# A fused decoder layer on one core: the opening's residual moved to ScalarE's queue, in a fixed order, with the first weight tiles in halves

## The chip, the cores and the metric

The kernel runs on one core of a Trainium2 chip. The metric is the device time of one launch in microseconds. A core has TensorE (matrix products, "PE"; its weight loads are listed as "PEld"), VectorE ("DVE"), ScalarE ("ACT"), GpSimd ("POOL") and SyncE ("SP"), which here only issues transfers. Each engine works through its own instructions in order and waits on semaphores; a transfer is issued by an engine's queue and carried out by 16 transfer engines that all queues share.

## What is computed

The reference is one inference step of a decoder layer over a group of 512 prompt tokens and 8 sequences of 8 sample tokens, 576 tokens in all, in float32. It has three sub-layers: a SwiGLU feed-forward block, a mixing block of attention and a state-space scan, and a second feed-forward block. The change lies ahead of and inside the first block:

```python
mod = (jax.nn.silu(c) @ w_ada + b_ada).reshape(bsz, N_SUB, 3, D_MODEL)
shift, scale, gate = mod[:, :, 0], mod[:, :, 1], mod[:, :, 2]
h = _modulate(x, g_pre[0], shift[:, 0], scale[:, 0])      # rms_norm(x, g) * (1 + scale) + shift
f = _swiglu(h, w_ffn_gate[0], w_ffn_up[0], w_ffn_down[0]) # (silu(h @ w_gate) * (h @ w_up)) @ w_down
x = x + FFN_RES * gate[:, 0][:, None] * rms_norm(f, g_post[0])
```

## The kernel before

Activations are kept with the 1024 features on partitions: `xT` is a tile of 128 partitions x 8 feature blocks x 576 tokens, worked on in two halves of 288 tokens (`HALF`). Products in float32 are made from three products of rounded parts: an operand is split into hi (a cast, on ScalarE) and lo (the remainder, a subtraction on VectorE or GpSimd), and `mm3` multiplies hi by hi, hi by lo and lo by hi. A weight tile `wraw` of 128 x 1024 is loaded by SP, cast to `whi` and subtracted to `wlo` by `weights()` (L148 on). That function counts its calls in `wcount`, and where `pool_weights` is set, which holds for the middle of the kernel, it gives the lo part of every second tile to GpSimd.

The opening works towards the first products of the first feed-forward block. SP loads `cT`, constants `cst`, the first half of `xT` in 8 pieces, three small constants, and then the conditioning weights `wada`, 8 pieces of 128 x 512 for each half of a modulation vector. The squares of `xT` are summed over the feature blocks (ScalarE squares, GpSimd adds, VectorE makes the last addition), a product with ones adds them over the partitions, and root and reciprocal follow in `rnorm`. Meanwhile `ada_half(1, 0, 2)` (L338 on) multiplies silu(c) by half of the scale's weights, in eight groups of four small products, transposes the result and writes the factors `A0` for four feature blocks. `prescale` (L463 on) then makes a scaled tile `pm` per feature block on VectorE, its cast `xh` on ScalarE and its remainder `xl` on VectorE or GpSimd.

`Split.half0` loads and splits the first three weight tiles whole, calls `then` (in the code `second`: the other half of the scale, the other four feature blocks, and sixteen steps of `shift`), and runs the 72 products of the three tiles, feature block by feature block. `shift` is a thread of its own: it loads the second half of `xT` and makes the 16 groups of products of the shift vector. Further weight tiles follow through `gemm` (L203 is its product line).

The order of each engine's instructions is set by a scheduler, which places what is not inside a block of `in_order()` by its own choice; inside such a block the order of the code holds between the block's own instructions. The order of SP's loads is the order in which the code calls `load`. The transfers' semaphores go round in eight, so that an issue can only go out when the transfer eight before it has landed.

Of the kernel before, what the change touches and what calls it, by code (L numbers as in the profile page):

```python
# [8 lines left out]
F32 = mybir.dt.float32  # L9
F32R = mybir.dt.float32r  # L10
# [26 lines left out]
def _layer(ctx, tc, A, O, tap, stop):  # L37
# [24 lines left out]
    def load(out, in_):  # L62
        in_queue([nc.sync.dma_start(out=out, in_=in_).ins])  # L63
# [40 lines left out]
    def const(name, shape, dt=F32, src=None):  # L104
        t = cp.tile(shape, dt, tag=name, name=name)
        load(t, A[name] if src is None else src)
        return t

    def f32(ap):
        return ap.bitcast(F32)  # L110

    def sub(out, a, b, pool=False):
        (G if pool else V).tensor_tensor(out, a, b, ALU.subtract)  # L113
# [25 lines left out]
    def run(g):  # L139
        for _ in g:  # L140
            pass
# [156 lines left out]
    class Split:  # L298
# [7 lines left out]
        def half0(self, first=True, last=True):  # L306
            if first:
                flush()
            kc, xh, xl, few = self.kc, self.xh, self.xl, self.first
            self.w = w = [weights(src, kc) for src, _ in self.tiles[:few]]  # L310
            if self.then:
                self.then()
            if few:
                ps = [mmt() for _ in range(few)]
                for k in range(kc):
                    for n in range(few):
                        mm3(ps[n][:, :HALF], *w[n][k], xh(k, 0), xl(k, 0), k == 0, k == kc - 1)
                for n in range(few):
                    self.tiles[n][1](0, 0, ps[n][:, :HALF])
            n0 = len(self.tiles) - self.keep  # L320
            for n, (src, evac) in enumerate(self.tiles[few:], few):
                w.append(weights(src, kc, n0 - self.far <= n < n0 or n in self.spare))
                gemm(None, kc, xh, xl, evac, (0,), w=w[-1])
                yield
            if last:
                flush()
# [127 lines left out]
            V.reciprocal(self.ps, self.ps)  # L454
            return self.ps

    def xsums(x, i):
        o = i * HALF
        s = Sums(NQ)
        for q in range(NQ):  # L460
            s.add(x[:, q, o:o + HALF])
        return s

    def prescale(x, rb, Aj, xh, xl, qs):

        for q in qs:
            t = tmp("pm")
            V.scalar_tensor_tensor(t, x[:, q, :HALF], Aj[:, q, 0:1], rb, ALU.mult, ALU.mult)
            S.copy(xh[:, q, :HALF], t)
            sub(xl[:, q, :HALF], t, f32(xh[:, q, :HALF]), q % 2 == 1)  # L470

    def premod(x, rb, Aj, j, xh, xl, i):

# [256 lines left out]
    load(cT, A["cT"])  # L730
    sq_c = cp.tile([128, 8, 32], F32, tag="sq_c", name="sq_c")
    S.activation(sq_c, cT, AF.Silu)
    cst = const("cst", [128, 448])
    ident, ones = cst[:, 0:128], cst[:, 128:256]
    smask, smask_s = cst[:, 256:384], cst[0:64, 384:448]
    xT, _ = xtile(F32, "xT")
    for q in range(NQ):
        load(xT[:, q, :HALF], A["xT"][:, q, :HALF])
    bada = const("b_ada", [128, 9, 8])
    gpre = const("g_pre", [128, 3, 8])  # L740
    gpost = const("g_post", [128, 3, 8])
    eps_t = cp.tile([128, 1], F32, tag="eps", name="eps_t")
    V.memset(eps_t, EPS)
    identb = cp.tile([128, 128], BF16, tag="identb", name="identb")
    V.tensor_copy(identb, ident)
    A0 = cp.tile([128, 8, 9], F32, tag="A0", name="A0")
    (xh, xhs), (xl, xls) = xtile(F32R, "xh"), xtile(F32R, "xl")
    rbs = [xsums(xT, 0).rnorm(1024.0)]
    run(ada_half(1, 0, 2))
    prescale(xT, rbs[0], A0, xh, xl, range(4))  # L750


    Gs, As = {}, {}
# [38 lines left out]
        V.tensor_tensor(xls[:, :, T:], sh, f32(xhs[:, :, T:]), ALU.subtract)  # L792
        yield from premod(xT, rbs[1], A0, 0, xh, xl, 1)

    def second():

        run(ada_half(1, 1))
        prescale(xT, rbs[0], A0, xh, xl, range(4, 8))
        for _ in range(PRES):
            next(shifts)  # L800
# [4 lines left out]
    look[0] = 1  # L805
    shifts = shift()
    wa = Blocks(xh, xl, lambda q: A["xT"][:, q:q + 2])
    ff = ffn(0, xh, xl, side(), last, wa, 3, (second, again()))
    merge((next(ff), 1), (shifts, SHIFT))
    end = next(ff)  # L810
    xh, xl = X2s
# [1370 lines left out]
```

## Time and profile before

| what | us |
|---|---|
| median of three runs | 1968.27 |
| lowest and highest run | 1964.12, 1970.24 |
| the profiled execution, its own time | 1972.4 |
| its span, first to last instruction | 1970.6 |
| TensorE busy in the span | 1888.8 (96%) |
| VectorE, ScalarE, GpSimd busy | 1433.0, 1027.1, 642.6 |

The busy times are those of the whole span; the opening is the first of 40 slices of it, some 49 us each. In the timeline rows the first two numbers are the start and the duration in us, then engine, line, operation, tiles and shapes, the count of merged instructions, and in brackets the idle time of the engine ahead of them with what ended it.

### The profile page before, as it was taken

The numbers are of one execution on the slowest core, as the hardware profiler recorded it, in microseconds if no ns is written. First come the engines' busy times: TensorE is split into PE (matmuls) and PEld (weight loads), VectorE is DVE, ScalarE is ACT, GpSimd is POOL, SyncE is SP. The second block draws the span as 40 slices with busy tenths as digits, with TensorE's granted clock in tenths as the row PEclk, the third lists the DMA queues.
The fourth block names the chain that finished last, engine by engine and source line by source line (L and its number), as shares of the span: only waits on it lengthen the run. The fifth ranks groups of instructions, "written<-read, shape, count | busy, mean of one in ns | idle before, by whom it ended". The sixth has DMA issues, their size and how long they took to land. (4 is left out here: it accounts for less than half of the span.)

```text
span 1970.6 us, 37005 instructions
## 1 busy us (share of the span) xinstructions
PE 1888.8 (96%) x13779; PEld 1747.8 (89%) x13779; DVE 1433.0 (73%) x2595; ACT 1027.1 (52%) x2247; POOL 642.6 (33%) x645
## 2 busy tenths in 40 slices
PE   6999999999999999999999999999988999999997
PEld 5999898998998999999899778777688999999997
DVE  4887577867785786677667667788866895766875
ACT  4655343556554565455434555655646754534553
POOL 1314234425553242333233111133332422332523
PEclk9999999998999999999999999999999999999999
DMA  9433546354544538355634444378847543232252
GB/s 324 147 111 128 193 134 198 100 188 143 169 133 153 150 95 248 106 174 150 206 120 155 159 138 147 110 259 272 292 164 254 179 166 92 80 100 89 86 178 80
DMA packets 171958, 313.84 MB, mean 159 GB/s; under 512 B 18129, under 2 KB 84402, under 8 KB 171778
## 3 DMA queue, kind: packets, MB, share of 16 engines
q1 hardware_dynamic: 145794, 268.98, 42.6%
q0 software_dynamic: 9088, 34.11, 4.9%
q10 hardware_dynamic: 16896, 8.39, 1.5%
q8 instruction: 108, 1.77, 0.4%
q14 instruction: 72, 0.59, 0.1%
HBM read 284.59 MB, written 26.83 MB: 158 GB/s over the span
## 5 line engine op out<-in xcount | busy, mean ns | idle before, releaser
L113 DVE TENSOR_TENSOR wlo<-wraw,whi 128x512 fp32r<-128x512 f32 (+2 forms) x300 | 336.9, 1126 | 124.7 <-ACT whi L167 94.8
L167 ACT CAST whi<-wraw 128x1024 fp32r<-128x1024 f32 (+2 forms) x264 | 238.0, 905 | 248.1 <-PE mm L203 133.1
L203 PE MATMUL mm<-xh,whi 128*128 128x288 f32 (+1 forms) x1368 | 344.1, 301 | 5.9 <-ACT xh L494 4.4
L203 PE MATMUL mm<-xl,whi 128*128 128x288 f32 (+1 forms) x1368 | 340.8, 298 | 3.2 <-DVE xl L484 2.6
L203 PE MATMUL mm<-xh,wlo 128*128 128x288 f32 (+1 forms) x1368 | 338.1, 296 | 0.2 <-DVE wlo L113 0.2
L203 PEld LDWEIGHTS mm<-xh,whi 128*128 128x128 f32 x1368 | 236.3, 190 | 14.3 <-ACT xh L494 4.6
L203 PEld LDWEIGHTS mm<-xl,whi 128*128 128x128 f32 x1368 | 236.5, 189 | 4.9 <-DVE xl L484 3.3
L203 PEld LDWEIGHTS mm<-xh,wlo 128*128 128x128 f32 x1368 | 236.6, 190 | 0.9 <-DVE wlo L113 0.4
L113 POOL TENSOR_TENSOR wlo<-wraw,whi 128x1024 fp32r<-128x1024 f32 (+1 forms) x60 | 122.0, 2034 | 213.5 <-ACT whi L167 191.3
L203 PE MATMUL mm<-hl,whi 128*128 128x288 f32 x640 | 161.2, 296 | 0.0
L203 PE MATMUL mm<-hh,whi 128*128 128x288 f32 x640 | 160.3, 295 | 0.0
L203 PE MATMUL mm<-hh,wlo 128*128 128x288 f32 x640 | 158.4, 295 | 0.0
L264 PE MATMUL mm<-t,whi 128*128 128x288 f32 x768 | 154.0, 295 | 0.2 <-ACT sg L612 0.2
L264 PE MATMUL mm<-xl,whi 128*128 128x288 f32 x512 | 150.6, 296 | 0.0
L264 PE MATMUL mm<-xh,wlo 128*128 128x288 f32 x512 | 149.0, 295 | 1.5 <-DVE wlo L113 1.5
L264 PE MATMUL mm<-xh,whi 128*128 128x288 f32 x512 | 147.9, 296 | 1.2 <-ACT u L281 0.8
L113 DVE TENSOR_TENSOR wlo<-area,whi 128x512 fp32r<-128x512 f32 x128 | 121.7, 965 | 12.2 <-ACT whi L239 11.6
L264 PEld LDWEIGHTS mm<-t,whi 128*128 128x128 f32 x768 | 122.9, 188 | 2.1 <-ACT whi L239 0.8
L441 POOL TENSOR_TENSOR acc<-acc,sq 128x288 f32<-128x288 f32 x72 | 70.0, 974 | 140.3 <-ACT sq L440 114.1
L203 PEld LDWEIGHTS mm<-hl,whi 128*128 128x128 f32 x640 | 110.8, 188 | 3.5 <-issue 3.4
L203 PEld LDWEIGHTS mm<-hh,whi 128*128 128x128 f32 x640 | 110.6, 188 | 3.5 <-ACT whi L167 1.7
L264 PE MATMUL mm<-t,wlo 128*128 128x288 f32 x384 | 112.6, 295 | 0.0
(443 smaller groups left out, 4666.7 us busy)
## 6 DMA issues: line engine op xcount, KB each, us to landing
wraw<-w_gu SPq DMA_DIRECT2D x108, 512.0 KB, 3.5
craw<-cache SPq DMA_DIRECT2D x128, 320.0 KB, 4.3
wraw<-w_in SPq DMA_DIRECT2D x72, 512.0 KB, 4.4
wada<-w_ada SPq DMA_DIRECT2D x80, 256.0 KB, 4.4
area<-w_ada POOLq DMA_DIRECT2D x16, 1024.0 KB, 6.0
wraw<-w_dn SPq DMA_DIRECT2D x24, 512.0 KB, 4.4
wraw<-w_dn SPq DMA_DIRECT2D x32, 256.0 KB, 2.6
M<-cscr SPq DMA_DIRECT2D x32, 256.0 KB, 4.6
```

What stands on the lines that cost most here:

```text
L113: (G if pool else V).tensor_tensor(out, a, b, ALU.subtract)
L167: S.copy(hi[:, :n], raw[:, :n])
L203: PE.matmul(p[:, :m.shape[-1]], a, m, start=(k == 0 and n == 0), stop=(k == kc - 1 and n == 2))
L264: PE.matmul(ps, l, r, start=(start and j == 0 and n == 0), stop=(stop and j == self.kc - 1 and n == 2), skip_group_check=True)
L441: (G if self.pool and not last else V).tensor_tensor(self.acc, self.acc, s, ALU.add)
```

## The change

The residual's first half and `cst` are issued by ScalarE's queue, in four pieces of two feature blocks, and not by SP's; SP issues the eight conditioning pieces right behind `cT` (`ada_half(1, 0, 8)`, all eight ahead). The six inner additions of the squares and all remainders of the first four scaled tiles go to VectorE. An `in_order()` block fixes the order of the first conditioning groups and the sums, another one that of the first four scaled tiles, alternating with the first halves of the three weight tiles; each of these tiles is now loaded, cast and subtracted in two halves of 128 x 512, written out in `half0` without a call of `weights()`. The second halves are made by `chunks(4)`, which `second` runs between the fifth and the sixth of its conditioning loads, outside of a fixed order.

```diff
             kc, xh, xl, few = self.kc, self.xh, self.xl, self.first
-            self.w = w = [weights(src, kc) for src, _ in self.tiles[:few]]
             if self.then:
-                self.then()
+                self.w = w = [[] for _ in range(few)]
+                bufs = [[wp.tile([128, 8, 128], dt, tag=t, name=t, bufs=b)
+                         for dt, t, b in ((F32, "wraw", 3), (F32R, "whi", 4), (F32R, "wlo", 4))] for _ in range(few)]
+
+                def chunks(k0):
+                    ks = slice(k0, k0 + 4)
+                    for (src, _), (raw, hi, lo), out in zip(self.tiles, bufs, w):
+                        load(raw[:, ks], src[:, k0 * 128:k0 * 128 + 512].rearrange("p (k m) -> p k m", m=128))
+                        S.copy(hi[:, ks], raw[:, ks])
+                        sub(lo[:, ks], raw[:, ks], f32(hi[:, ks]))
+                        out += [(hi[:, k], lo[:, k]) for k in range(k0, k0 + 4)]
+                        yield
+                with in_order():
+                    merge((self.then[0](), 1), (chunks(0), 1))
+                self.then[1](chunks(4))
+            else:
+                self.w = w = [weights(src, kc) for src, _ in self.tiles[:few]]
...
-    def xsums(x, i):
+    def xsums(x, i, pool=True):
         o = i * HALF
-        s = Sums(NQ)
+        s = Sums(NQ, pool=pool)
...
-    def prescale(x, rb, Aj, xh, xl, qs):
+    def prescale(x, rb, Aj, xh, xl, qs, pool=True):
...
-            sub(xl[:, q, :HALF], t, f32(xh[:, q, :HALF]), q % 2 == 1)
+            sub(xl[:, q, :HALF], t, f32(xh[:, q, :HALF]), pool and q % 2 == 1)
...
-    cst = const("cst", [128, 448])
+    cst = cp.tile([128, 448], F32, tag="cst", name="cst")
+    nc.scalar.dma_start(out=cst, in_=A["cst"])
...
-    for q in range(NQ):
-        load(xT[:, q, :HALF], A["xT"][:, q, :HALF])
-    bada = const("b_ada", [128, 9, 8])
-    gpre = const("g_pre", [128, 3, 8])
-    gpost = const("g_post", [128, 3, 8])
+    for q in range(0, NQ, 2):
+        nc.scalar.dma_start(out=xT[:, q:q + 2, :HALF], in_=A["xT"][:, q:q + 2, :HALF])
...
-    rbs = [xsums(xT, 0).rnorm(1024.0)]
-    run(ada_half(1, 0, 2))
-    prescale(xT, rbs[0], A0, xh, xl, range(4))
+    opening = ada_half(1, 0, 8)
+    for _ in range(8):
+        next(opening)
+    bada = const("b_ada", [128, 9, 8])
+    gpre = const("g_pre", [128, 3, 8])
+    gpost = const("g_post", [128, 3, 8])
+    with in_order():
+        for _ in range(6):
+            next(opening)
+        rbs = [xsums(xT, 0, False).rnorm(1024.0)]
+
+    def first():
+
+        run(opening)
+        for q in range(4):
+            prescale(xT, rbs[0], A0, xh, xl, (q,), False)
+            yield
...
-    def second():
+    def second(more):
 
-        run(ada_half(1, 1))
+        opening = ada_half(1, 1, 4)
+        for _ in range(5):
+            next(opening)
+        run(more)
+        run(opening)
         prescale(xT, rbs[0], A0, xh, xl, range(4, 8))
...
-    ff = ffn(0, xh, xl, side(), last, wa, 3, (second, again()))
+    ff = ffn(0, xh, xl, side(), last, wa, 3, ((first, second), again()))
```

What this does to ScalarE's order between the root of the sums and the squares of the second half is seen in the built programs. `xh` is one tile for all feature blocks, so its numbered sources `pm` tell the blocks apart; `wraw_198`, `wraw_201` and `wraw_204` are the three weight tiles, and DMAHW1 to DMAHW3 are the semaphores of their loads. Before:

```order
L453 ACTIVATE aux_130<-aux_130,eps_t_100 128x288 [waits PE_49]
L167 CAST whi_229<-wraw_228 128x1024 [waits DMAHW5_49]
L167 CAST whi_235<-wraw_234 128x1024 [waits DMAHW6_49]
L469 CAST xh_105<-pm_188 128x288 [waits DVE_49]
L167 CAST whi_241<-wraw_240 128x1024 [waits DMAHW7_49]
L469 CAST xh_105<-pm_192 128x288 [waits DVE_49]
L469 CAST xh_105<-pm_196 128x288 [waits DVE_49]
L469 CAST xh_105<-pm_200 128x288 [waits DVE_49]
```

And in the changed program:

```order
L468 ACTIVATE aux_169<-aux_169,eps_t_90 128x288 [waits PE_49]
L484 CAST xh_95<-pm_222 128x288 [waits DVE_49]
L319 CAST whi_199<-wraw_198 128x512 [waits DMAHW1_49]
L484 CAST xh_95<-pm_229 128x288 [waits DVE_49]
L319 CAST whi_202<-wraw_201 128x512 [waits DMAHW2_49]
L319 CAST whi_199<-wraw_198 128x512 [waits DMAHW1_49]
L319 CAST whi_202<-wraw_201 128x512 [waits DMAHW2_49]
L319 CAST whi_205<-wraw_204 128x512 [waits DMAHW3_49]
L484 CAST xh_95<-pm_236 128x288 [waits DVE_49]
L319 CAST whi_205<-wraw_204 128x512
L484 CAST xh_95<-pm_243 128x288 [waits DVE_49]
```

The first scaled tile's cast now stands ahead of the weights' casts. The second halves of all three tiles (the second appearance of `whi_199` and `whi_202`, and the first of `whi_205`) stand between the first halves of the second and the third tile, ahead of the third scaled tile.

SP's queue from its first issue to the first weight tile, where `w_ada0` are the conditioning weights. Before:

```order
L63 DMA cT_79<-cT 128x256
L63 DMA cst_83<-cst 128x448
L63 DMA xT_85<-xT 128x288 x6
L63 DMA xT_85<-xT 128x288 [waits DMAHW0_49]
L63 DMA xT_85<-xT 128x288 [waits DMAHW1_49]
L63 DMA b_ada_94<-b_ada 128x72 [waits DMAHW2_49]
L63 DMA g_pre_96<-g_pre 128x24 [waits DMAHW3_49]
L63 DMA g_post_98<-g_post 128x24 [waits DMAHW4_49]
L63 DMA wada_135<-w_ada0 128x512 [waits DMAHW5_49]
```

And in the changed program, where the four pieces of `xT` on ScalarE's queue raise DMAHW3, DMAHW5, DMAHW7 and DMAHW1:

```order
L63 DMA cT_79<-cT 128x256
L63 DMA wada_98<-w_ada0 128x512
...
L63 DMA wada_106<-w_ada0 128x512 [waits DMAHW2_49]
L63 DMA wada_108<-w_ada0 128x512 [waits DMAHW3_49]
L63 DMA wada_110<-w_ada0 128x512 [waits DMAHW4_49]
L63 DMA wada_112<-w_ada0 128x512 [waits DMAHW5_49]
L63 DMA b_ada_114<-b_ada 128x72 [waits DMAHW6_49]
L63 DMA g_pre_116<-g_pre 128x24 [waits DMAHW7_49]
L63 DMA g_post_118<-g_post 128x24 [waits DMAHW0_49]
L63 DMA wraw_198<-w_gu 128x512 [waits DMAHW1_49]
```

The residual has left the queue, the conditioning weights stand at its head, and the first weight tile, now a half, waits for the semaphore that the last piece of `xT` raises.

## Rows read from the trace of the kernel before

**Rows 1.** The page: busy tenths of TensorE in 40 slices of the span.

```profile
PE   6999999999999999999999999999988999999997
```

**Rows 2.** Stretches: busy us of each engine, granted clock, DMA share, GB/s.

```profile
2.00:9.00 7.00, 0.00 (x0) 0.00 (x0) 0.23 (x1) 3.80 (x11) 2.53 (x4) 1.00 0.87 248
9.00:14.00 5.00, 2.08 (x18) 1.28 (x22) 0.67 (x2) 1.67 (x2) 2.21 (x3) 1.00 0.98 331
14.00:19.00 5.00, 2.38 (x56) 1.83 (x46) 3.35 (x6) 1.55 (x2) 0.00 (x0) 1.00 1.03 411
19.00:26.00 7.00, 5.54 (x38) 4.20 (x39) 6.44 (x9) 2.92 (x6) 2.23 (x2) 0.51 1.06 384
26.00:33.00 7.00, 7.00 (x98) 5.91 (x98) 4.48 (x10) 3.48 (x9) 1.76 (x2) 1.00 1.05 383
```

**Rows 3.** Timeline of the opening: start, us, engine, line, operation, idle before.

```profile
1.68 3.75 SPq L63 DMA_DIRECT2D xT<-xT  x8
...
6.19 5.18 POOL L441 TENSOR_TENSOR acc<-acc,sq 128x288 f32<-128x288 f32 x6 [5.74 <-ACT sq L440]
...
6.51 2.38 ACT L440 ACTIVATE sq<-xT 128x288 f32<-128x288 f32 x6 [0.40 <-DMA xT<-xT]
...
11.40 0.46 DVE L441 TENSOR_TENSOR acc<-acc,sq 128x288 f32<-128x288 f32 x1 [7.04 <-POOL acc L441]
...
11.91 1.33 PE L430 MATMUL aux<-acc,cst 128*128 128x288 f32 x2 [11.91 <-DVE acc L441]
...
13.17 3.21 PE L350 MATMUL aux<-wada,sq_c 128*32 128x128 f32 x64
...
13.28 0.47 ACT L453 ACTIVATE aux<-aux,eps_t 128x288 f32<-128x288 f32 x1 [3.09 <-PE aux L430]
...
13.79 1.97 DVE L454 RECIPROCAL aux<-aux 128x288 f32<-128x288 f32 x1 [1.93 <-ACT aux L453]
...
17.21 1.04 ACT L167 CAST whi<-wraw 128x1024 fp32r<-128x1024 f32 x1 [3.46 <-DMA wraw<-w_gu]
...
17.24 0.20 DVE L360 TENSOR_TENSOR A<-A,g_pre 128x36 f32<-128x36 f32 x1
...
18.29 1.23 DVE L113 TENSOR_TENSOR wlo<-wraw,whi 128x1024 fp32r<-128x1024 f32 x1 [0.85 <-ACT whi L167]
...
19.43 1.78 DVE L468 SCALAR_TENSOR_TENSOR pm<-xT,A,aux 128x288 f32<-128x288 f32 x4
...
20.46 0.85 PE L173 MATMUL mm<-xh,whi 128*128 128x288 f32 x2 [4.08 <-ACT xh L469]
```

**Rows 4.** Timeline, VectorE and TensorE later in the first three tiles.

```profile
30.53 1.89 DVE L113 TENSOR_TENSOR xl<-pm,xh 128x288 fp32r<-128x288 f32 x2
...
32.03 0.40 PE L174 MATMUL mm<-xl,whi 128*128 128x288 f32 x1
...
39.01 0.30 PE L174 MATMUL mm<-xl,whi 128*128 128x288 f32 x1
39.14 0.29 PE L175 MATMUL mm<-xh,wlo 128*128 128x288 f32 x1
```

**Rows 5.** DMA queues from 661 to 662 us (q1 is SP's, q10 ScalarE's).

```profile
q1 hardware_dynamic: 85, 0.33, 82.8%
q10 hardware_dynamic: 87, 0.04, 14.6%
```

**Rows 6.** DMA from 25 to 27 us.

```profile
DMA packets 651, 0.74 MB, mean 372 GB/s; under 512 B 38, under 2 KB 625, under 8 KB 650
```

**Rows 7.** Groups by shape: count, busy us, mean ns, idle before.

```profile
L113 DVE TENSOR_TENSOR wlo<-wraw,whi 128x1024 fp32r<-128x1024 f32 x133 | 174.5, 1313 | 63.3 <-ACT whi L167 63.0
...
L113 POOL TENSOR_TENSOR wlo<-wraw,whi 128x1024 fp32r<-128x1024 f32 x35 | 89.0, 2543 | 141.6 <-ACT whi L167 126.1 <-issue 14.5 <-POOL u L834 0.9
```

**Rows 8.** Waits of TensorE: us in total, times, longest.

```profile
PE mm L203 <- DVE wlo L113: 3.7, 5, 1.8
...
PE mm L203 <- POOL wlo L113: 1.7, 2, 1.2
```

## The prediction, made before the changed kernel ran

> **What bounds the kernel now.** I read the page first: in TensorE's row of 40 slices one stands far below the others, the first, with 6 tenths [rows 1]. The change edits only that slice, so the question is what the opening loses and how much of it comes back.
>
> Next the table of stretches [rows 2]. TensorE does nothing until 9 us, 2.08 us of work from 9 to 14, 2.38 from 14 to 19, and from 26 on it is full. In the last column the transfers run at 248 GB/s from 2 to 9, 331 from 9 to 14, and 383 to 411 from 14 to 33, where the DMA share stands above 1. The opening thus runs against two limits: TensorE's work, and a transfer stream that is saturated from 14 on.
>
> Then the timeline of the opening [rows 3]. The last six squares of the residual end at 8.89, but GpSimd's chain of six sums runs to 11.37; the last sum (11.40), the product with ones (11.91), the root (13.28) and the reciprocal (13.79 to 15.76) follow. The conditioning product ends at 16.38, so A0 is only complete at 17.44. VectorE then stands behind a whole weight tile: wlo from 18.29 to 19.52, after a cast that waited until 17.21 for its transfer. The first scaled tile is made from 19.43 to 19.88, and TensorE's first real product starts at 20.46. From there it never waits long, yet it is slow at first: over 19 to 26 it was granted 0.51 of its 2.4 GHz [rows 2]. The 72 products of the first three weight tiles start their last one at 39.14 [rows 4]. I call that point E and ask where it goes. Behind it the order of TensorE's instructions is the same through the first feed-forward block, and TensorE is the bound there, so I pass a shift of E on one for one.
>
> **Part by part.** *Residual from ScalarE.* SP spent 3.75 us issuing eight xT pieces [rows 3]; these issues leave its queue; ScalarE gets five, cst and four of two pieces each, the last three of them behind sq_c, which waits for cT. The weights of the conditioning start at once, so the stream saturates near 2 us. But the residual no longer has the transfer engines to itself. Before, its 1.54 MB (with cT and cst) were through near 8.2: 1.54 MB by 248 GB/s from 2.0. After, it shares them with 2.10 MB of w_ada0. How two queues share is shown where SP loads weights beside ScalarE's stores: in one microsecond 85 packets of the one and 87 of the other, 0.33 against 0.04 MB [rows 5]. They take turns by packet, whatever a packet's size. xT has 8 x 128 packets of 1152 bytes, w_ada0 has 8 x 128 of 2048, so both finish at about the same time: 3.64 MB by 372 GB/s (the rate while xT's second half loaded, [rows 6]) make 9.7 us, so 11.7, and 0.7 us until the semaphore. That 0.7 lies between at most 0.3 for xT (last square begun at 8.5, against 8.2) and 1.2 for the first weight tile (4.22 MB are through at 16.0, its cast starts at 17.21). So the last piece of xT lands at **L = 12.4**, against 8.5 or less. From below L is 8.9, if ScalarE's pieces were served first; from above 17.2, if 248 GB/s was the rate of the first microseconds itself and not SP's pace of issue.
>
> The Trainium skill (DMA: Bandwidth & Descriptors, "Issuing engines are not separate DMA queues") speaks against this part: transfers from all engines interleave on the same 16 engines, and issuing from a second one saves only sequencer time. By it alone the part would be worth no more than what SP's pace left unused from 2 to 9, 0.13 of 7 us or 0.9 us, and E would come at 38.2; the trace agrees as far as [rows 5] go.
>
> *Sums on VectorE.* Six GpSimd additions (5.18 us in a chain) become VectorE's, each under the next square. After L: two squares at 0.40 and one addition, 1.3 us; product 1.37, root 0.51, reciprocal 1.97, four small operations 1.0 (of the 1.06 from 16.38 to 17.44), first scaled tile 0.45 [rows 3]. It ends at P = L + 6.6 = 19.0. Cast and its gaps 0.58 (19.88 to 20.46), half a weight cast 0.55 (of 1.04): first product at 20.1, against 20.46. The fixed order takes out 2.0 us (17.44 to 19.43) and GpSimd's tail 2.5, and the later xT gives nearly all of it back.
>
> *Halved weight tiles.* The order listing shows what is not in the diff: the casts of all three second halves stand on ScalarE ahead of the third scaled tile, and their three subtractions on VectorE ahead of xl of that tile. From P to the end of xl of the fifth tile VectorE has, for each of the first two tiles, 0.5 us of waiting for the cast, xl 0.45 (as the addition), a half wlo 0.66 (a little over half of 1.23) and the next scaled tile 0.45: 4.2 us so far; three second halves 2.0; xl, wlo, scaled tile 1.55; A0's four small operations and an xl 1.5; four scaled tiles 1.8; xl beside GpSimd 0.95 (1.89 for two, [rows 4]). Sum 12.0, so it ends at 31.0. SP cannot undercut this: the first half tile waits on the semaphore of the last xT piece, so the stream pauses and resumes near L + 1.3 = 13.7; 2.88 MB on, at 384 GB/s, and 1.2 us of landing, the second halves are there at 22.4, when ScalarE reaches them at P + 3.3 = 22.3. Little time either way.
>
> *TensorE from there.* 33 products remain behind xl of the fifth tile, as in before at 32.03. Before, five groups of conditioning products lay among them up to 39.14; 32 steps of 0.13 (39.01 to 39.14) make 4.2, so a group costs 0.58. After, six lie there, since two run in the wait ahead (before: three). E = 31.0 + 4.2 + 6 x 0.58 = **38.7, some 0.5 us earlier**. The stream keeps up: the next whole weight tile, 8.3 MB after it resumes, lands near 36.5, ahead of E.
>
> *Clock.* At its lower level, 1.2 GHz, for most of 19 to 26 in before, after TensorE had stood from 16.38. Up to 31.0 the new order waits on VectorE, where a slow product costs nothing. If the low stretch outlives 31.0, each of 32 steps takes twice its 0.13, up to 4.2 us; if not, 0. I take 0, since TensorE gets products from 20.1, as early as in before.
>
> *A side effect.* weights() counts its calls and gives every second lo part to GpSimd in the middle of the kernel. The three first tiles no longer call it, so every later tile changes sides: GpSimd has 35 large and 25 half ones before, 37 and 23 after. A large one takes 2.54 us on GpSimd, 1.31 on VectorE [rows 7]. TensorE waited 1.7 us for GpSimd's in two places and 3.7 for VectorE's in five [rows 8]. From below: both gone, -5.4, though nothing frees all of them; nearer -2. From above: 1.23 us more at three of them, +4. The sides are symmetric, so I take 0.
>
> Sum: the profiled execution took 1972.4 us (the table above); less 0.5 is 1971.9. It lay 4.1 above the median of the three runs, so on their scale **1967.8 us**, no change that can be told: 0.3%, 5.9 us, is about what a measurement of this kernel tells from nothing.
>
> **Rivals.** *The residual comes early.* If xT is not held to equal turns, everything from P on hangs on L one for one, down to L = 8.9: E 4.0 us earlier, 1964.3. For: ScalarE's issues of pieces two to four can precede much of SP's queue, which waits on xT's semaphores. Against: [rows 5].
>
> *The residual comes late; slower.* Break-even is L = 12.9. At 248 GB/s throughout, 3.64 MB end at 16.5 and L is 17.2: E 4.3 us later, 1972.6. For: 9 to 14 us still had 331 although SP had issued ahead. Against: the DMA share of 0.87 from 2 to 9 leaves room. A clock that stays low through the 33 products would look alike in the time, up to +4.2.
>
> *The halves buy nothing, and the swap decides.* E within 0.5 us, and the kernel moves by what GpSimd's tiles do in the middle of the kernel, -2 to +4: 1966 to 1972.
>
> *All gains at once*: early residual and a lucky swap, 1962.
>
> **How the numbers follow.** Forecast (within 2 us of 1967.8) 0.50; early residual 0.22; late residual or long low clock 0.16; the halves worth nothing and the swap beyond 2 us, either way, 0.12. Only an early residual together with the swap passes 5.9 us: faster 0.11. Slower needs late and swap together: 0.06. Same 0.83. The range runs from the lower end of early and swap, 1961.5, to just past late, 1973.
>
> **What would show it.** Right: the last squares end near 13 instead of 8.89, the sums of squares reach TensorE near 13.7, its first real product is near 20; a pause in the transfers near 13; casts of second halves ahead of the third scaled tile; the third scaled cast near 24.5; E near 38.7; GpSimd's wlo on other tiles, the span otherwise shifted evenly. Wrong: xT complete before 11, E before 37, or a stage behind the first block whose length moves by more than 2 us.

## The result: the opening came forward, the kernel became 0.6% slower

The changed kernel took 1979.67 us (median of 13 runs, 1975.42 to 1984.16), the one before 1969.25 (13 runs): a ratio of 1.0062, with an interval from 1.0051 to 1.0073. The profiled execution has a span of 1976.9 us, against 1970.6. The forecast was 1967.8, no change.

The opening is not where it was lost. These are the stretches of the kernel after that answer to [rows 2]:

```profile
2.00:9.00 7.00, 2.29 (x32) 0.83 (x32) 0.69 (x2) 2.13 (x4) 0.00 (x0) 1.00 0.99 336
9.00:14.00 5.00, 2.32 (x26) 0.90 (x18) 2.75 (x6) 3.61 (x7) 0.00 (x0) 1.00 0.99 335
14.00:19.00 5.00, 3.25 (x42) 1.21 (x40) 3.26 (x7) 0.95 (x3) 0.00 (x0) 1.00 0.98 339
19.00:26.00 7.00, 6.76 (x64) 4.61 (x56) 6.33 (x12) 3.85 (x9) 0.00 (x0) 1.00 1.05 370
```

TensorE now works from 5.5 us on. The view gives 1.00 as its granted clock in 19 to 26, where it gave 0.51 before, but that is no gain of a level: the trace's record of the clock begins only at 24.12 us here, and at 15.68 before, and where there is no record the view counts 1.00. The products tell the level. Those of 128x288 begin 0.24 us apart up to 23.65, as in the low stretch of before, and 0.13 apart later:

```profile
23.41 0.44 PE L174 MATMUL mm<-xl,whi 128*128 128x288 f32 x1
23.65 0.44 PE L175 MATMUL mm<-xh,wlo 128*128 128x288 f32 x1
...
27.25 0.29 PE L173 MATMUL mm<-xh,whi 128*128 128x288 f32 x1
27.38 0.30 PE L174 MATMUL mm<-xl,whi 128*128 128x288 f32 x1
```

And before:

```profile
24.99 0.44 PE L174 MATMUL mm<-xl,whi 128*128 128x288 f32 x1
25.23 0.44 PE L175 MATMUL mm<-xh,wlo 128*128 128x288 f32 x1
...
28.03 0.29 PE L174 MATMUL mm<-xl,whi 128*128 128x288 f32 x1
28.17 0.29 PE L175 MATMUL mm<-xh,wlo 128*128 128x288 f32 x1
```

So the lower level, 1.2 GHz, ends at about 24.1 us, where before it ended at 25.9. The timeline of the changed opening, for [rows 3, 4]:

```profile
1.18 0.45 ACTq L754 DMA_DIRECT2D xT<-xT  x1
...
3.88 1.42 ACTq L754 DMA_DIRECT2D xT<-xT  x3
...
11.66 0.78 ACT L455 ACTIVATE sq<-xT 128x288 f32<-128x288 f32 x2 [0.64 <-DMA xT<-xT]
...
13.23 1.33 PE L445 MATMUL aux<-acc,cst 128*128 128x288 f32 x2 [0.20 <-DVE acc L456]
...
15.10 1.97 DVE L469 RECIPROCAL aux<-aux 128x288 f32<-128x288 f32 x1 [1.93 <-ACT aux L468]
...
17.98 0.51 DVE L483 SCALAR_TENSOR_TENSOR pm<-xT,A,aux 128x288 f32<-128x288 f32 x1
...
19.53 0.61 PE L173 MATMUL mm<-xh,whi 128*128 128x288 f32 x1 [0.24 <-ACT whi L319]
...
37.88 0.40 PE L175 MATMUL mm<-xh,wlo 128*128 128x288 f32 x1
```

The last piece of the residual lands by 11.66, the first scaled tile is ready at 18.49, the first real product starts at 19.53 (20.46 before) and the last of the 72 at 37.88 (39.14 before): 1.3 us gained. The eight profiles of this opening, counted with the experiments below, bear it out: the last of the 72 starts at 37.9 on the mean (36.7 to 38.8), and at 39.2 (38.4 to 40.1) in the four profiles of the opening before. Paired product by product, TensorE is about 1.2 us ahead from 65 to 200 us.

Then it stands still for longer than before. In 480 to 535 us, 600 to 720, 880 to 905, 1060 to 1130 and 1585 to 1612 TensorE waits 3.0, 3.0, 2.0, 4.8 and 3.7 us, where the kernel before has 2.5, 1.8, 0.6, 2.2 and 1.9. The waits of the kernel after in these five places (engine, operation, what it waited for: us in total, times, longest):

```profile
PE mm L203 <- ACT xh L498: 2.1, 1, 2.1
PE mm L203 <- DVE xl L499: 0.5, 1, 0.5
PE mm L203 <- ACT u L869: 0.4, 1, 0.4
...
PE aux L1090 <- DVE H L1144: 2.8, 2, 2.5
...
PE aux L1204 <- DVE sn L1206: 1.6, 3, 0.6
PE aux L1204 <- ACT tg L912: 0.4, 1, 0.4
...
PE mm L203 <- DVE qll L1515: 1.6, 1, 1.6
PE mm L1664 <- DVE kt L1583: 1.4, 1, 1.4
PE mm L1664 <- DVE qf L1619: 1.2, 1, 1.2
PE mm L1609 <- POOL wlo L113: 0.6, 1, 0.6
...
PE mm L203 <- ACT sg L659: 3.0, 2, 1.9
PE mm L203 <- DVE xl L499: 0.7, 1, 0.7
```

Only one of these waits is for a weight's lo part. The others are for VectorE's chains (H of the state, qll and qf of the queries) or for ScalarE behind them. At four of the five places a stretch at the lower clock lies beside the waits, as the windows show (after the stretch: us, busy us of PE, PEld, DVE, ACT, POOL, then the granted clock, DMA share, GB/s):

```profile
502.20:505.60 3.40, 3.20 (x14) 3.20 (x15) 0.51 (x2) 0.68 (x2) 1.68 (x2) 0.53 0.02 5
707.00:710.40 3.40, 3.12 (x14) 3.12 (x15) 3.40 (x8) 3.33 (x10) 2.24 (x4) 0.53 0.26 77
894.80:901.60 6.80, 6.31 (x27) 6.24 (x27) 5.22 (x20) 1.05 (x1) 0.00 (x0) 0.52 0.92 263
1597.90:1601.30 3.40, 3.40 (x17) 3.40 (x16) 3.40 (x7) 0.87 (x2) 1.77 (x2) 0.53 0.50 153
```

The profile of the kernel before has such stretches too, at other places; its mean granted clock is 0.984, against 0.987 here. This pair of profiles therefore does not show that the clock is where the kernel lost.

### The profile page after: what moved, and what is told of

Same layout as the page of the kernel before. It is cut to its first block, busy times and chain, and to the rows that moved or that the text cites. A ratio compares the mean times of both kernels' runs of the same rounds, so it can differ in the third digit from the quotient of the medians.

```text
span 1976.9 us, 36993 instructions
## 1 busy us (share of the span) xinstructions
PE 1890.5 (96%) x13779; PEld 1746.4 (88%) x13779; DVE 1440.2 (73%) x2606; ACT 1026.3 (52%) x2250; POOL 630.9 (32%) x637
## 4 chain that ended last, share of the span: by engine, by line
PE 45%; DVE 10%; ACT 3%; DMA 3%; issue 2%; POOL 1%; SPq 0%; DVEq 0%; ACTq 0%; POOLq 0%
PE mm L203 25%; PE mm L264 8%; PE mm L1609 2%; DVE wlo L113 1%; PE aux L1885 1%; DMA wraw<-w_gu 1%; DVE kp L113 1%; PE mm L174 1%; PE aux L1682 1%; ACT whi L167 1%; POOL cwlo L113 1%; DVE xbc L882 1%; PE mm L175 1%; DVE small L1858 1%; PE aux L1126 1%
## 5 line engine op out<-in xcount | busy, mean ns | idle before, releaser
L203 PE MATMUL mm<-xh,whi 128*128 128x288 f32 (+1 forms) x1368 | 346.8, 304 | 13.2 <-ACT xh L509 4.4
L203 PE MATMUL mm<-xl,whi 128*128 128x288 f32 (+1 forms) x1368 | 342.3, 299 | 2.5 <-DVE xl L499 1.8
L203 PE MATMUL mm<-xh,wlo 128*128 128x288 f32 (+1 forms) x1368 | 339.6, 297 | 0.4 <-DVE wlo L113 0.4
L203 PEld LDWEIGHTS mm<-xh,whi 128*128 128x128 f32 x1368 | 238.3, 192 | 22.5 <-ACT xh L509 4.6
L203 PEld LDWEIGHTS mm<-xl,whi 128*128 128x128 f32 x1368 | 238.4, 191 | 4.0 <-DVE xl L499 2.5
L203 PEld LDWEIGHTS mm<-xh,wlo 128*128 128x128 f32 x1368 | 238.4, 191 | 1.0 <-DVE wlo L113 0.9
L203 PE MATMUL mm<-hl,whi 128*128 128x288 f32 x640 | 161.2, 296 | 0.0
L203 PE MATMUL mm<-hh,whi 128*128 128x288 f32 x640 | 160.5, 296 | 0.0
L203 PE MATMUL mm<-hh,wlo 128*128 128x288 f32 x640 | 158.5, 296 | 0.0
L264 PE MATMUL mm<-t,whi 128*128 128x288 f32 x768 | 154.0, 295 | 0.2 <-ACT sg L627 0.2
L264 PE MATMUL mm<-xl,whi 128*128 128x288 f32 x512 | 150.6, 296 | 0.0
L264 PE MATMUL mm<-xh,wlo 128*128 128x288 f32 x512 | 148.9, 295 | 0.7 <-DVE wlo L113 0.7
L264 PE MATMUL mm<-xh,whi 128*128 128x288 f32 x512 | 148.0, 296 | 0.9 <-ACT u L281 0.9
L264 PEld LDWEIGHTS mm<-t,whi 128*128 128x128 f32 x768 | 123.1, 188 | 2.1 <-issue 0.8
L203 PEld LDWEIGHTS mm<-hl,whi 128*128 128x128 f32 x640 | 110.9, 188 | 3.5 <-issue 3.4
L203 PEld LDWEIGHTS mm<-hh,whi 128*128 128x128 f32 x640 | 110.7, 188 | 3.7 <-ACT whi L167 1.7
L264 PE MATMUL mm<-t,wlo 128*128 128x288 f32 x384 | 112.8, 295 | 0.0
L247 POOL TENSOR_TENSOR area<-wraw 128x512 f32<-128x512 f32 x32 | 48.6, 1518 | 196.5 <-DVE t L113 95.8
```

The costliest lines, as they stand in the source:

```text
L203: PE.matmul(p[:, :m.shape[-1]], a, m, start=(k == 0 and n == 0), stop=(k == kc - 1 and n == 2))
L247: G.tensor_tensor(s1, b[:, 0], b[:, 1], ALU.add)
L264: PE.matmul(ps, l, r, start=(start and j == 0 and n == 0), stop=(stop and j == self.kc - 1 and n == 2), skip_group_check=True)
```

## The experiments

The first theory was the side effect that the prediction had set to zero: the lo parts of the weight tiles changed sides between VectorE and GpSimd. The rival was that the opening itself displaces what follows.

**Restoring the sides, flipping them alone, and taking the opening apart.**

```diff
 e1_parity, e8_parity_again (the changed kernel, line added under "if self.then:")
+                wcount[0] += few
 e2_flip (the kernel before)
-    wcount = [0]
+    wcount = [1]
 e3_parity_sp (e1_parity, and)
-    nc.scalar.dma_start(out=cst, in_=A["cst"])
+    load(cst, A["cst"])
-        nc.scalar.dma_start(out=xT[:, q:q + 2, :HALF], in_=A["xT"][:, q:q + 2, :HALF])
+        load(xT[:, q:q + 2, :HALF], A["xT"][:, q:q + 2, :HALF])
 e4_parity_whole, e15_whole_again (e1_parity, and in chunks)
-                        load(raw[:, ks], src[:, k0 * 128:k0 * 128 + 512].rearrange("p (k m) -> p k m", m=128))
+                        if k0 == 0:
+                            load(raw, src[:, 0:1024].rearrange("p (k m) -> p k m", m=128))
 e5_whole (e4_parity_whole without wcount[0] += few)
```

> The changed kernel with one line more: the count that picks VectorE or GpSimd for a weight tile's lo part is raised by three where the three opening tiles no longer raise it, so every later tile has the side that it had before the change; the opening stays as changed. Theory (the swap of sides): products run ahead of before by about 1.2 us after the opening, as in the changed kernel, and the three losses of 3 to 5 us near 500, 707 and 895 us are gone; 1967 to 1970 us, ratio to before 0.998 to 1.001. If the loss near 1590 us stays, which lies behind the end of GpSimd's share, 1970 to 1972 and 1.001 to 1.002. Rival (the earlier opening itself displaces the later order and the clock): the losses stay, 1977 to 1981 us, 1.004 to 1.006.

> The kernel before with one number changed: the count starts at 1, so every weight tile in GpSimd's stretch changes side and nothing in the opening changes. Theory (the swap): stalls of 3 to 5 us near 501, 708 and 895 us, 1976 to 1981 us, ratio 1.0035 to 1.006, without any change in the opening. Rival (the opening displaces what follows): as before, 1967 to 1971, within 0.15%.

> As e1_parity, but the residual and cst are issued from SyncE again, in their place ahead of the conditioning weights. If ScalarE's queue brings the opening's gain, the first real product comes at about 20.5 us again (19.5 in the changed kernel) and the time is about 1 us above e1_parity. Rival (the fixed order and the halves bring it): first product within 0.3 us of 19.5, time within 0.5 us of e1_parity.

> As e1_parity, but each of the first three weight tiles comes in one transfer of 128x1024, while casts and subtractions stay halves. If the halves bring the products forward, the first product is later by what a half of 128x512 takes to move and the time is 0.5 to 1.5 us above e1_parity. Rival (scaled tiles end last at the first product): first product and the products of the fifth tile within 0.3 us of e1_parity's.

> The changed kernel with each of the first three weight tiles in one transfer of 128x1024 instead of two halves; the sides of the lo parts stay swapped. So it differs from e4_parity_whole by the swap alone. Theory (the swap costs the same with any opening, as it did between the changed kernel and e1_parity: 7.9 us): 1973 to 1976 us, ratio 1.002 to 1.0035. Rival (what the scheduler makes of each opening behind 430 us decides, and the swap is worth about 2 us as in e2_flip): 1967 to 1970, 0.999 to 1.0005.

> e1_parity once more, the same program, for a second set of runs and a second profile. In the first profile a weight tile of the last stage of the first block landed late at 324 us beside a transfer of w_ada by GpSimd's queue, and TensorE lost about 3 us there. If that belongs to the program: again a wait of 1.5 us or more there, and 1970 to 1974 us. If it was chance: no such wait, and 1966 to 1970 us.

> e4_parity_whole once more, the same program (sides as before, whole transfers), the best of the set. If its 1966.3 us and the absence of waits between 480 and 535 us belong to the program: 1964 to 1967.5 us, ratio to before 0.998 to 0.9995, no wait above 0.3 us there. If they were the chance of one set of runs: 1968 to 1972 us.

**GpSimd's share taken out, or begun later.** In e6_allv (the changed kernel) and e7_allv_before (the kernel before) the share is never switched on. In e9_late_parity, e10_late_after, e11_late_before and e12_late_whole (from e1_parity, the changed kernel, the kernel before and e4_parity_whole) the switch moves:

```diff
 e6, e7
-    pool_weights[0] = True
+    pool_weights[0] = False
 e9 to e12
-    pool_weights[0] = True
     st = steps()
...
     run(st)
+    pool_weights[0] = True
```

> The changed kernel with GpSimd's share of the lo parts never switched on: all of them on VectorE, so there are no sides to swap. VectorE has 60 more subtractions of 1.2 us in the stretch from 480 to 1470 us. Theory (the swap is the loss): within 0.15% of e7_allv_before, whatever both stand at. Rival (the opening and the order that follows from it lose it): 3 us or more above e7_allv_before.

> The kernel before with GpSimd's share never switched on. It is there for e6_allv to be measured against. If VectorE has room for 60 subtractions of 1.2 us beside the products: within 0.2% of before. If it has none: up to 1.2 us for each that stands in a wait, 5 to 40 us more.

> e1_parity with GpSimd's share of the lo parts switched on later: behind the small steps of the time constants (about 530 us) instead of ahead of the products that begin at 480 us. In e1_parity a GpSimd subtraction of 2.4 to 2.8 us at 516.5 us stands beside four small VectorE instructions of 128x160 that take 2.4 to 2.5 us each instead of 0.3, and TensorE then waits 2.8 us for their result; another wait of 0.9 us is at 505 us. Theory (GpSimd's subtraction holds VectorE, and the place of the hold is what costs): these instructions take 0.3 us, the wait is gone, 1966 to 1969 us. Rival (the order alone, holds or not): 1971 to 1973 us as in e1_parity.

> The changed kernel, sides swapped, with GpSimd's share switched on later as in e9_late_parity. Theory: the loss at 499 us (a wait of 2.1 us for the scaled tile behind a VectorE instruction held from 495 to 498 us) is gone, the four later places (707, 893, 1064 to 1127 and 1595 us) keep theirs, 6 to 7 us in all by the profile: 1973 to 1977 us. Rival (the loss at the beginning of the share is most of it): within 2 us of e9_late_parity.

> The kernel before with the later switch, for the others of this set to be measured against. Theory: its own wait of 1.9 us at 530 us goes, 1966 to 1968 us, 0 to 0.1% below before. Rival: no change.

> e4_parity_whole (whole transfers, sides as before) with the later switch. e4_parity_whole has no wait at the places in question, so the theory expects no gain: 1964 to 1967 us, ratio to before 0.998 to 0.9995. If it comes out above 1968, what the scheduler makes of each program weighs as much as any hold.

**One tile alone.**

```diff
 e13_one_off (the changed kernel)
-        pool = wcount[0] % 2 == 0 and pool_weights[0]
+        pool = wcount[0] % 2 == 0 and pool_weights[0] and wcount[0] != 160
 e14_one_on (e1_parity)
-        pool = wcount[0] % 2 == 0 and pool_weights[0]
+        pool = (wcount[0] % 2 == 0 or wcount[0] == 163) and pool_weights[0]
```

> The changed kernel with the lo part of one weight tile, the 160th call, put on VectorE; it is the GpSimd subtraction that runs at 1077.4 us for 2.40 us. Beside it VectorE's ckl (128x288) took 2.44 us and its cnl (128x64) 2.63 us behind it, 0.46 and 0.21 us where GpSimd is idle, and TensorE waited 1.6 us for qll at 1084 us. Theory (the GpSimd subtraction holds VectorE, the chain to qll is late by that): both take under 1 us, the wait for qll goes or falls below 0.5 us, the other places stay; the time falls by 1 to 3 us, 1977 to 1979. Rival (the order on VectorE makes the wait): the wait stays above 1.2 us.

> The converse: e1_parity with the lo part of that one tile (its 163rd call) on GpSimd, where e1_parity has it on VectorE and no wait for qll. It is the first call whose side differs between the two; the others keep theirs. The scheduler's order changes in a few rows there and in some 60 of VectorE and 54 of ScalarE at about 1560 to 1610 us, where no tile has changed side. Theory (hold): a wait of about 1.6 us for qll comes in at about 1080 us. If the order behind it matters too, the wait for sg at about 1595 us rises from 0.5 to about 3 us in the same run. 1973 to 1976 us. Rival (order of VectorE alone): no wait for qll above 0.5 us.

**What was measured.** The ratio is to the kernel before in the same set of runs. The column of waits adds up what the view of TensorE's waits gives for 480 to 535, 600 to 720, 880 to 905, 1060 to 1130 and 1585 to 1612 us of one profile; before it is 9.0. These places were picked because the changed kernel falls back there. Over the whole span the view gives it 73.5 us and the kernel before 69.3.

| kernel | sides | opening | us | ratio, interval | waits, us |
|---|---|---|---|---|---|
| changed kernel | swapped | changed | 1979.67 | 1.0062, 1.0051 to 1.0073 | 16.5 |
| e5_whole | swapped | whole transfers | 1980.00 | 1.0072, 1.0057 to 1.0088 | 16.3 |
| e10_late_after | swapped, later | changed | 1977.72 | 1.0056, 1.0035 to 1.0078 | 14.6 |
| e13_one_off | swapped but one | changed | 1980.17 | 1.0067, 1.0050 to 1.0084 | 17.8 |
| e2_flip | swapped | before | 1971.34 | 1.0018, 1.0004 to 1.0032 | 12.6 |
| e14_one_on | before but one | changed | 1971.78 | 1.0017, 1.0005 to 1.0029 | 14.6 |
| e1_parity | before | changed | 1971.81 | 1.0015, 1.0000 to 1.0030 | 10.5 |
| e8_parity_again | before | changed | 1971.77 | 1.0028, 1.0013 to 1.0042 | 10.1 |
| e9_late_parity | before, later | changed | 1969.22 | 1.0006, 0.9988 to 1.0023 | 7.5 |
| e12_late_whole | before, later | whole transfers | 1972.21 | 1.0020, 1.0005 to 1.0034 | 7.4 |
| e11_late_before | before, later | before | 1968.82 | 1.0004, 0.9992 to 1.0017 | 7.8 |
| e6_allv | none | changed | 1968.72 | 1.0008, 0.9998 to 1.0018 | 8.0 |
| e7_allv_before | none | before | 1966.49 | 0.9998, 0.9987 to 1.0008 | 8.0 |
| e3_parity_sp | before | residual on SP | 1967.36 | 0.9989, 0.9974 to 1.0003 | 6.2 |
| e4_parity_whole | before | whole transfers | 1966.30 | 0.9986, 0.9972 to 0.9999 | 4.9 |
| e15_whole_again | before | whole transfers | 1967.13 | 0.9986, 0.9973 to 1.0000 | 5.3 |

*Against what was expected.* In the first set only e1_parity came out inside its theory, by the branch with 1970 to 1972 us. e2_flip fell between theory and rival, close to the rival. e3_parity_sp and e4_parity_whole have the first product later than e1_parity (20.56 and 20.36 against 20.16), but 4.5 and 5.5 us less time, where more was expected. e5_whole lies above either range. e6_allv and e7_allv_before came as in theory. e8_parity_again has no stretch at the lower clock near 324 us and a wait of 1.4 us there, yet repeats the time of e1_parity. e9_late_parity and e10_late_after lie 0.2 and 0.7 us above the range of the theory. e11_late_before has 0.9 us of waits at the first place, where before has 2.5, and no gain in time. e12_late_whole missed its range by 5 us. e13_one_off and e14_one_on showed the wait as in theory and missed the time. e15_whole_again came as expected.

*The swap is the loss.* With the changed opening it costs 7.9 us (the changed kernel against e1_parity, medians of two sets; by the ratios 6.7 to 9.2, with e8_parity_again) and 8.5 (e10_late_after against e9_late_parity, one set); with whole transfers 13.7 (e5_whole against e4_parity_whole, two sets; by the ratios 16.9). Without GpSimd's share there is nothing to swap, and the changed kernel is back within 0.1% of before and 2.2 us above e7_allv_before. So the rival fell as the main cause. The theory was too simple as well: with the opening of before the swap costs only 2.2 us (e2_flip), and e1_parity stays 0.15 to 0.28% above before though its sides are those of before.

*The waits sort the kernels.* The swapped kernels have 12.6 to 17.8 us of waits at the five places, the others but e14_one_on 4.9 to 10.5. At three of the places the swap adds with every opening: 1.3 to 1.5 us in 880 to 905, 2.6 in 1060 to 1130, 1.1 to 2.3 in 1585 to 1612. In 600 to 720 it adds 1.1 to 1.9, but nothing with the opening of before. In 480 to 535 us, where the products of w_in begin, each program stands differently: 3.0 us in the changed kernel, 3.7 in e1_parity and again in e8_parity_again, none in e4_parity_whole and e15_whole_again, 2.5 before, 0.3 in e2_flip. The last two are why the swap looked cheap there: it gave back 2.2 us at this place. In all, the swap adds 3.6, 6.0, 7.1 and 11.4 us of waits at the five places in the four pairs in which it costs 2.2, 7.9, 8.5 and 13.7 us. Over the whole span it adds less, 2.1, 3.2, 3.2 and 8.4, so that part of the loss does not stand in these waits.

*The clock's part.* From each run's span and granted clock, span times what the clock lacks to 1 is 27.4 us on the mean of the changed kernel's runs and 21.8 in e4_parity_whole; the remainder is 1951.1 against 1942.1. Of the 14.8 us between their means 9.0 are work and waits at the full clock, 5.6 the lower clock, and 0.2 lies outside the span. e4_parity_whole is among the lowest; the four swapped kernels with a new opening lose 25.3 to 27.4 us to the clock, the nine others with a new opening 20.6 to 24.3. (With the opening of before the record takes in the low stretch at 19 us, so those kernels can't be set beside them.) That the waits bring the lower clock about is not shown: e14_one_on has 14.6 us of waits and loses only 22.2.

*What makes the waits.* The changed kernel around 1080 us, VectorE and GpSimd:

```profile
1075.89 0.46 DVE L1505 TENSOR_TENSOR ckl<-ckf,ckh 128x288 fp32r<-128x288 f32 x1
...
1077.43 2.40 POOL L113 TENSOR_TENSOR wlo<-wraw,whi 128x1024 fp32r<-128x1024 f32 x1 [0.75 <-ACT whi L167]
...
1077.70 2.44 DVE L1505 TENSOR_TENSOR ckl<-ckf,ckh 128x288 fp32r<-128x288 f32 x1 [0.51 <-ACT ckh L1504]
...
1080.07 2.63 DVE L1540 TENSOR_TENSOR cnl<-ckf,cnh 128x64 fp32r<-128x64 f32 x1
1080.36 1.57 POOL L456 TENSOR_TENSOR acc<-acc,sq 128x288 f32<-128x288 f32 x2
1081.88 0.73 POOL L113 TENSOR_TENSOR wk<-wraw,wk 128x256 fp32r<-128x256 f32 x1
...
1084.67 0.40 PE L203 MATMUL mm<-xh,whi 128*128 128x288 f32 x1 [1.59 <-DVE qll L1515]
```

The subtraction ckl takes 0.46 us at 1075.89; the same shape beside GpSimd's wlo ends about when that ends, after 2.44. cnl, a quarter of the width, takes 2.63; it stands beside what GpSimd does next, two additions and wk, and ends with them. qll stands behind both, and TensorE waits for qll. With this one tile on VectorE (e13_one_off), in a program whose rows on VectorE and ScalarE otherwise come in the same order:

```profile
1078.61 1.23 DVE L113 TENSOR_TENSOR wlo<-wraw,whi 128x1024 fp32r<-128x1024 f32 x1 [0.23 <-ACT whi L167]
...
1079.76 1.07 DVE L1505 TENSOR_TENSOR ckl<-ckf,ckh 128x288 fp32r<-128x288 f32 x1
1080.75 0.82 DVE L1540 TENSOR_TENSOR cnl<-ckf,cnh 128x64 fp32r<-128x64 f32 x1
```

The two still take longer than alone, beside GpSimd's additions, but the wait for qll is gone from the view. With the one tile on GpSimd in a kernel that has the other sides (e14_one_on) it comes in:

```profile
1069.09 2.40 POOL L113 TENSOR_TENSOR wlo<-wraw,whi 128x1024 fp32r<-128x1024 f32 x1 [0.92 <-ACT whi L167]
1069.37 2.44 DVE L1506 TENSOR_TENSOR ckl<-ckf,ckh 128x288 fp32r<-128x288 f32 x1 [0.67 <-ACT ckh L1505]
1071.74 2.64 DVE L1541 TENSOR_TENSOR cnl<-ckf,cnh 128x64 fp32r<-128x64 f32 x1
...
1076.33 0.40 PE L203 MATMUL mm<-xh,whi 128*128 128x288 f32 x1 [1.63 <-DVE qll L1516]
```

So at this place a GpSimd subtraction holds VectorE's small ones, shown both ways. Which instructions are held can be counted over the profiles, between 480 and 1480 us. Beside a 128x1024 subtraction on GpSimd xbc<-u,conv_w,xbc takes 2.87 us instead of 0.84 (medians, eight times in the changed kernel). But sn<-sn,dcol,aux takes 0.34 in all its eight places, as elsewhere, and osm<-osm,mm 0.45 as elsewhere: these read one input, aux or mm, from where TensorE writes its products. The kernel before has such holds as well (xbc six times, median 2.85); what the swap changes is where they fall. e1_parity shows it at 516 us too: u<-u,tok of 128x160 takes 2.52 us beside a wlo of 2.82 us on GpSimd, where neighbours of that shape take 0.31; TensorE then waits 2.8 us for rest, the end of that chain. In e9_late_parity, with the share begun later, that wait is gone; the time is 2.6 us lower, which the intervals don't tell from nothing.

```profile
515.97 0.31 DVE L965 TENSOR_SCALAR u<-aux 128x160 f32<-128x160 f32 x1
516.47 2.82 POOL L113 TENSOR_TENSOR wlo<-wraw,whi 128x1024 fp32r<-128x1024 f32 x1 [0.60 <-ACT whi L167]
516.95 2.52 DVE L966 TENSOR_TENSOR u<-u,tok 128x160 f32<-128x160 f32 x1
...
522.12 0.31 DVE L970 TENSOR_TENSOR u<-u 128x160 f32<-128x160 f32 x1
```

*The order comes with it.* In e14_one_on the wait for sg near 1590 us is 2.0 us against 0.5 in e1_parity, as far behind the tile as 500 us and after GpSimd's share has ended (its last subtraction begins at 1473 us in the changed kernel). The scheduler that puts the instructions in order had placed some 60 of VectorE's rows there otherwise. The whole swap moves about 180 of its 2606. TensorE's row behind that wait, in e1_parity and in e14_one_on:

```profile
1592.53 0.40 PE L203 MATMUL mm<-xh,whi 128*128 128x288 f32 x1 [0.50 <-ACT sg L660]
...
1586.98 0.40 PE L203 MATMUL mm<-xh,whi 128*128 128x288 f32 x1 [1.95 <-ACT sg L660]
```

*What stays open.* How the swap's cost divides between holds and order is not shown. One place does not show in the time: e13_one_off lost a wait of 1.6 us and stands at 1980.17, where 1977 to 1979 was expected, but its interval of 1.0050 to 1.0084 is too wide to tell 1.6 us; at two other places its profile has 1.6 and 1.7 us more of waits than the changed kernel's, with the same order. e14_one_on gained some 4 us of waits in its profile and stands at e1_parity's time. And e12_late_whole has few waits at the five places and is 5 to 6 us above e4_parity_whole and e15_whole_again, of which 2.5 to 3.7 is the lower clock. So the sum of waits sorts the kernels, but does not add up to the time one by one; single profiles, in which the low stretches fall differently, don't settle why.

*The opening by itself.* The start of TensorE's 400th product, over all the profiles: 51.9 us on the mean of four kernels with the opening of before (51.2 to 52.8), 50.8 in eight with the changed one (49.6 to 51.7), 52.4 in four with whole transfers (51.6 to 53.7), 53.5 in the one with the residual on SP. So the change brings 1.2 us; without the halves it comes 1.6 later, without ScalarE's queue 2.8 later, in one profile. The end of the lower clock moves along: by the start of the record and the steps of the products it lies at 22.3 to 26.1 us in the eight, at 31.3 in e3_parity_sp. These worths hold the clock's part in them, and the runs don't separate it. The best kernels of all, e4_parity_whole and e15_whole_again, lack the gain of the halves: 0.14% below before in two sets, both intervals at or just under 1.

## Why the prediction was wrong, by its steps

- **L, the landing of the residual, and P.** Forecast 12.4 and 19.0; last squares begun at 11.66, first scaled tile ready at 18.49. Between the equal turns that I chose and the early bound, nearer to the turns: right in kind, 0.5 to 0.7 us late in size. (The late bound has a slip: 3.64 MB by 248 GB/s from 2.0 end at 16.7, not 16.5.) The rule that a second issuing engine saves only sequencer time (the Trainium skill, DMA: Bandwidth & Descriptors, "Issuing engines are not separate DMA queues") gave 0.9 us for this part. e3_parity_sp has the 400th product 2.8 later, but this one profile does not test the rule: its clock rises only at 31.3 us, and its last squares are done by 9.2 while the product with ones starts at 13.75, behind conditioning products that the fixed order puts first.
- **First product and E.** Forecast 20.1 and 38.7, measured 19.53 and 37.88. That is 1.3 us gained where 0.5 was forecast: the right sign, with the size small against the scatter of 2 us between profiles of one opening. The halves were sized at little time either way; the 400th product comes 1.6 us later without them. The casts of the second halves do run ahead of the third scaled tile (its xh at 23.08, forecast 24.5), and no wait for a transfer precedes them.
- **Clock.** I took a slow product to cost nothing up to 31.0. The lower level did stay, and ended by 26.1 in the eight profiles of this opening, so the 4.2 us that I feared behind 31.0 did not come. But nothing is too little: where it ended by 22.9 (three profiles) the last of the 72 products starts 17.5 to 17.9 us behind the first, where it lasted to 23.9 to 26.1 (five) 18.2 to 18.7.
- **A shift of E passes on one for one, and the order behind is the same.** I read the order only through the first feed-forward block. From 430 us on the scheduler orders differently for each opening, and 480 to 535 us holds between 0 and 3.7 us of waits accordingly. This is the first step that failed. e1_parity and e8_parity_again are 2.7 and 4.7 us above before with the same sides, although their opening is ahead; that the waits at 480 to 535 us make this is likely, but not shown.
- **The side effect, taken as 0 between -2 and +4.** This is the step that failed most: it measured +8 to +9 with the changed opening, and that is what took the time out of the range. I priced a lo part by its length on the two engines, 2.54 against 1.31 us, and by TensorE's waits for wlo itself [rows 7, 8]. The 5.4 us of [rows 8] are those of line L203; with 1.5 at L264 they were 6.9, and 6.5 after. So the term that I priced did not grow at all. The price lay elsewhere: GpSimd's 2.4 us hold those instructions of VectorE beside it that read two inputs from SBUF, and the swap of all sides brings a new order too. What TensorE then waits for has other names: qll, for which e13_one_off and e14_one_on show the hold; H and xh, behind VectorE rows of 4.79 us for three and 3.08 us for two beside such a subtraction, which no run tests alone (e1_parity has 4.63 for the three, and no wait above 0.4 us there); and sg, which the order alone moves in e14_one_on. "The sides are symmetric" holds for the counts of tiles, not for the places.
- **What was to show it.** The text named "a stage behind the first block whose length moves by more than 2 us" as a sign of being wrong. That came: from 496 to 506 us alone TensorE fell back by 4.2. "E before 37" came in two of the eight profiles (36.7 and 36.9).

The rule that would have told me stands in the Trainium skill, SBUF — State Buffer, "Who interferes with whom": a VectorE instruction with two inputs in SBUF and a GpSimd instruction that reads SBUF take turns on a shared pair of ports, and the later one is blocked for the whole length of the other. This case's rows agree: 2.44 us instead of 0.46 beside a subtraction of 2.40, and 0.34 as ever where one input is a product of TensorE's.

## What to carry to other kernels

A count or a parity that spreads work over two engines is part of every edit that changes how often it is called: look up which instruction lands on which engine at every place behind the edit, or tie the choice to the tile instead of to the call. Price work moved to GpSimd by the VectorE chain that runs beside it, those instructions above all that have both inputs in SBUF, and look for the damage in waits that bear other names. When a scheduler orders the program, compare the order to its end before passing a gain in the opening on one for one: 1.2 us won in the opening weighed less here than what was dealt anew at 500.

## What the runs showed of the hardware

- A GpSimd subtraction of 128x1024 takes 2.40 us and holds a 128x288 subtraction on VectorE for 2.44 us (0.46 alone); one of 2.82 us holds a 128x160 for 2.52 (0.31). A VectorE instruction of which one input is a product of TensorE's is not held: sn<-sn,dcol,aux takes 0.34 us in all eight such places.
- GpSimd's share of the lo parts brings nothing here: with all 60 tiles on VectorE the kernel before measured 0.9998 (0.9987 to 1.0008), although VectorE was given 60 subtractions more.
- The view's granted clock reads 1.00 also where the trace has no record of it: in the changed opening up to 24.12 us, while products of 128x288 begin 0.24 us apart, as at the granted clock of 0.50 to 0.55 before, and 0.13 apart later.
- At four places TensorE's waits have 3.4 to 6.8 us at a granted clock of 0.52 to 0.53 beside them; that a wait brings them about is not shown.
